# Hybrid GLA and GDN block: five GDN heads instead of six in the transposed form, the norm's row through GpSimd's queue, and its product a tick later

## The chip, the cores and the metric

The kernel runs on one core of a Trainium2 chip. The metric is the device time of one execution in microseconds (us), the median of several runs. One core has a matrix engine (TensorE, called PE below), a vector engine (VectorE, DVE), a scalar engine (ScalarE, ACT), GpSimd (POOL) and SyncE (SP). SP, ACT and POOL each issue DMAs, and 16 DMA engines move the bytes.

## The reference

The block computes, for one sequence of 1024 tokens of width 1024, a gated linear attention (GLA) of 4 heads and a gated delta rule (GDN) of 8 heads on the same normalised input, projects each with its own weight, merges the two by sigmoid gates, projects again, and ends with a squared-ReLU MLP. All is float32. What matters here is the end of the GDN part:

```python
def rms_norm(x, w):
    xf = x.astype(jnp.float32)
    y = xf * lax.rsqrt(jnp.mean(xf * xf, axis=-1, keepdims=True) + EPS)
    return (y * w.astype(jnp.float32)).astype(x.dtype)
...
    o_d = gated_delta_chunked(d_q, d_k, d_v.reshape(bsz, s, GDN_HEADS, GDN_DV), beta, g)
    o_d = rms_norm(o_d, gdn_onorm_w) * jax.nn.silu(d_g.reshape(bsz, s, GDN_HEADS, GDN_DV))
    y_d = o_d.reshape(bsz, s, GDN_V) @ w_branch_gdn
```

Each head's output o has 1024 tokens by 128 values. Its norm takes, for each token, the mean of the squares over the 128 values; then o is scaled, multiplied by the gate and given to the projection, which wants the values on the partitions and the tokens along the free axis.

## The kernel before, in words

**Matmuls.** PE carries nearly everything. A float32 product is split into a high and a low part (tiles with H and L in their names: hH, hL, wH, wL), and three matmuls take the place of one. `dense_b` (L477) makes one projection of 128 columns for all 1024 tokens: 8 k steps of 6 matmuls, accumulated in a tile pm of PSUM (128 x 1024). Small products go to tiles pa (128 x 512). The GLA projection, the gate projection and the GDN projection (`branch`, one after another) each make seven products P2, P1, P6, P7, P4, P5, P3 of sums of quarters, in the manner of Strassen. The weight's quarters are called A11, A12, A21 and A22, and the input's Q11 to Q22.

**The agenda.** A clock counts ticks: one after each k step of `dense_b`, and one after each two k steps of a `branch` product. `at(dt, fn)` (L373) puts a function on the agenda dt ticks later, and `tick` (L384) runs what is due. In a GDN head `on(t, fn)` counts from the head's first tick, and `last_on(t, fn)` puts the function behind everything else of that tick. PE, DVE and ACT execute what they are given in just this order. From head 7 on, POOL's instructions and SP's DMAs keep the order of the code too (the loop that calls `gdn_head`, L1852 on, sets `strict` for them); before that the scheduler places them by what they wait for.

**A GDN head.** `gdn_head(h)` (L909) takes 24 ticks: three `dense_b` (for q, v and the gate). It starts a recurrence over 8 chunks at tick 24 (`c0`, `c1`, `c2`: PE multiplies ke with the state st, ACT makes rs and vn, DVE makes the next st from decB and a pa tile), which lasts to about tick 48. So a head's tail runs on ticks 48 and later, beside the next heads' first projections, and head 7's recurrence runs beside the first products of the GLA projection. In the code, `begin` is the head's first tick, so tick 50 of head 5 is tick 2 of head 7.

**Two forms of the tail.** The flag `turned` (L979) chooses.

- Turned, heads 0 to 5: `c2` writes o with the values on the partitions, which is how the projection wants it. The sums over values are then sums over partitions: ACT squares (`half_squares`, ticks 48 and 50), DVE transposes in 32 x 32 blocks and reduces (`sums`, 53 and 56), the groups are added (`groups`, 59), and `roots` (62) makes 1024 reciprocal roots in a 32 x 32 tile sqt and stores them, 4 KB, to `on_d[h]` in DRAM. `rows` (66) reads them back as a broadcast to all 128 partitions: the tile row, 512 KB. `gated` (58) has multiplied o into the gate sg (the tile si), and `times` (71) multiplies sg by row on DVE. Three ticks behind, ACT's queue stores sg to `od_d` (512 KB).
- Not turned, heads 6 and 7: o has the tokens on the partitions. ACT squares with a running sum (`results`, ticks 35 and 47), PE and DVE make the token sums of q in another place (`token_total`, tick 32, with the constant quad; its columns vq at tick 33), `norm` (48) makes a column rs of 8 numbers a partition, `scale` (50) multiplies the tile ob, and `fin` (52, 53) turns ob by eight PE transposes (`pa<-ident,ob`), which DVE multiplies into sg. The store to `od_d` is on tick 56. For head 6 these ticks are moved back by `end` = 27 and more (L1076), for head 7 the last ones by 6.

**Load buffers.** Most tiles of 512 KB share one pool of 30 buffers, which are given out in rotation (tag w4, L24): row, si, ob, aacc's input araw, the xq and wq tiles, and others. A load into a buffer waits until the tile that was there before is done with.

**The GLA projection's loads.** `gla_plan` (L1653) lists ticks relative to the end of head 7: SP loads the weight quarter A12, then Q21, A11, Q11, Q12, Q22 (each xq pair 2 x 512 KB) and A21 (the tiles wq, 2 x 512 KB) on ticks -19 to -2, and A22 on tick 8. On tick 1 `add_w` adds A22 onto A21 in SBUF by two DMAs of POOL's queue, which must follow SP's load of A21. On ticks 8 and 10 DVE subtracts A11 from the sum (`raw<-wq,raw`). `w_neg` (ticks -9 to 2) fills the low halves of the weights, tiles wB, by four more DMAs of POOL's queue.

Of the kernel before, what the change touches and what calls it, by code (L numbers as in the profile page):

```python
# [50 lines left out]
def block_kernel(ctx: ExitStack, tc: tile.TileContext, x, c, ada_w, ada_b, pre_mix_w, post_mix_w,  # L51
# [15 lines left out]
    V, A, G, T = engines = [InOrder(tc, e) for e in (nc.vector, nc.scalar, nc.gpsimd, nc.tensor)]  # L67
    DMA, ST = InOrder(tc, nc.sync), nc.scalar
# [8 lines left out]
    def t4(shape=(128, 1024), dt=F32, p="t", tag="w4"):  # L77
        return w4.tile(list(shape), dt, tag=tag, name=nm(p), bufs=tag_bufs[tag])
# [7 lines left out]
    def dump(name, src, dst=None):  # L86
        if dbg and name in dbg:
            DMA.dma_start(dbg[name] if dst is None else dst(dbg[name]), src)


    def rsqrt(v, n, rt=None):

        if rt:
            r, t = rt
        elif n == 64:
            r, t = t4((128, n), p="rs"), t4((128, n), p="rt")
        else:
            r, t = small(n, "rs"), small(n, "rt")
        V.tensor_scalar(t.bitcast(I32), v.bitcast(I32), 1, None, ALU.logical_shift_right)
        V.tensor_scalar(r.bitcast(I32), t.bitcast(I32), -1.0, float(0x5F3759DF), ALU.mult, ALU.add)  # L100

        V.tensor_mul(t, r, r)
        V.tensor_mul(t, t, v)
        V.scalar_tensor_tensor(t, t, -10.0 / 3, t, ALU.add, ALU.mult)
        V.scalar_tensor_tensor(r, t, 5.0, r, ALU.add, ALU.mult)
        V.tensor_mul(t, r, r)
        V.scalar_tensor_tensor(t, t, -27.0 / 1024, v, ALU.mult, ALU.mult)
        last["rs"] = V.scalar_tensor_tensor(r, t, 9.0 / 16, r, ALU.add, ALU.mult).ins
        return r

    def small(n, p="s", bufs=3, dt=F32):
        return sm.tile([128, n], dt, tag=f"{p}{n}", name=nm(p), bufs=bufs)
# [260 lines left out]
    def at(dt, fn):  # L373
        agenda.append((clock[0] + dt, len(agenda) + uid[0] * 100000, fn))
        agenda.sort(key=lambda e: e[:2])
        uid[0] += 1
# [324 lines left out]
    def r3(t, n=8):  # L701
        return t.rearrange("p (t q) -> p t q", t=n)
# [203 lines left out]
    od_d = [dr.tile([2, 128, 1024], F32, name=f"od_d{i}") for i in range(4)]  # L906
    on_d = [dr.tile([1024], F32, name=f"on_d{h}") for h in range(8)]

    def gdn_head(h, then=None):  # L909
# [3 lines left out]
        def on(t, fn):  # L913
            at(begin + t - clock[0], fn)
# [38 lines left out]
        def conv_silu(ps, ct, t, late=0):  # L953

            y, u = t4(p="cv"), {}
            A.activation(y, ps, AF.Copy, scale=ccol[:, 3 * 24 + ct:3 * 24 + ct + 1])

            def tap(s_):
                V.scalar_tensor_tensor(y[:, s_:], ps[:, :S - s_], ccol[:, (3 - s_) * 24 + ct:(3 - s_) * 24 + ct + 1],
                                       y[:, s_:], ALU.mult, ALU.add)  # L960

            def tanh():
                u["t"] = t4(p="si")
                A.activation(u["t"], y, AF.Tanh)

            t += late
            for s_ in (1, 2, 3):
                on(t + s_, lambda s_=s_: tap(s_))
            on(t + 4, tanh)
            on(t + 6 - late, lambda: V.scalar_tensor_tensor(y, u["t"], 1.0, y, ALU.add, ALU.mult))  # L970
            return y
# [4 lines left out]
        psq = dense_b(h_rhs)  # L976

        q = conv_silu(psq, h, 8)
        z, turned = {}, h < 6  # L979
        vq = None if turned else small(8, "vq")  # L980

        def att(hf):
# [52 lines left out]
        c = {"st": None}  # L1035
# [81 lines left out]
        def sums(hf):  # L1117
            if not hf:
                c["t"] = t4(p="sqt")
            h_ = slice(hf * 512, (hf + 1) * 512)  # L1120
            V.transpose(c["t"][:, h_], c["sq"][:, h_])
            V.reduce_sum(so[:, hf * 16:(hf + 1) * 16], r3(c["t"][:, h_], 16), axis=mybir.AxisListType.X)
# [11 lines left out]
        def roots():  # L1134
            g = c["g"]
            V.transpose(g[5], rsqrt(g[0], 32, g[3:5]))
            DMA.dma_start(on_d[h].rearrange("(b i) -> b i", i=32), g[5])

        def rows():
            c["row"] = t4(p="row")  # L1140
            DMA.dma_start(c["row"], on_d[h].partition_broadcast(128))

        def gated():
            V.scalar_tensor_tensor(sg, c["ob"], don, sg, ALU.mult, ALU.mult)

        def times():
            V.tensor_mul(sg, sg, c["row"])
            on(74, lambda: A.dma_start(od_d[h // 2][h % 2], sg))
            dump("odT", sg, lambda t: t[h * 128:(h + 1) * 128, :])

        def last_on(t, fn):
            on(t, lambda: at(0, fn))
# [6 lines left out]
            then()  # L1159
        if turned:  # L1160
            for t, fn in ((48, lambda: half_squares(0)), (50, lambda: half_squares(1)), (53, lambda: sums(0)),
                          (56, lambda: sums(1)), (58, gated), (59, groups), (62, roots), (66, rows), (71, times)):
                last_on(t, fn)
        else:
            on(48 + end, norm)
            on(50 + end, scale)
            on(52 + f_, lambda: fin(0))
            on(53 + f_, lambda: fin(1))
        psg = dense_b(h_rhs)

        sg = t4(p="si")
# [1251 lines left out]
    for n in range(len(seq)):  # L2423
        gi, key, c = seq[n]
# [106 lines left out]
```

## Time and profile before

| | |
|---|---|
| runs | 1894.22, 1892.55, 1894.04 us; median 1894.04 |
| profiled execution | 1894.02 us |
| its span in the trace | 1892.3 us |
| mean granted clock of PE | 0.997 |
| PE busy | 1862.0 us, 98% of the span |
| DVE busy | 1393.2 us, 74% |
| ACT busy | 887.7 us, 47% |
| POOL busy | 150.4 us, 8% |

The profiled execution took 1.7 us more than its span, the time outside the first and the last instruction. An engine that is busy for a smaller share may still be what PE waits for at one place. Row by row, a line of the profile gives a start, a duration, the engine, the operation, what it writes and reads, and in brackets how long the engine had been idle before and what ended the wait. Nearly all rows have the line L38, that of the helper which records every operation (`InOrder`), so the tiles' names tell the place. Tiles that matter: st, ke, rs, vn (the recurrence of a head), row and on_d (the norm's row), si (the gate), ob (a head's output), xq and wq (input and weight quarters of the GLA projection), raw (a whole weight piece), sl (the merge's gates, read from DRAM beside A22), wB (split weights), od_d (a head's result in DRAM).

### The profile page before, as it was taken

How to read it: one execution, taken by the hardware profiler on the slowest of the kernel's cores; microseconds unless marked ns; L12 is line 12 of the kernel's file. 1: busy time of each engine (PE TensorE's matmuls, PEld its weight loads, DVE VectorE, ACT ScalarE, POOL GpSimd, SP SyncE). 2: the span in 40 equal slices, each digit the busy share in tenths (PEclk: the TensorE clock that was granted, in tenths of full speed). 3: DMA queues.
4: the chain of work that ended last, by engine and by line, in shares of the span. 5: the costliest groups of instructions: out<-in, count | busy, mean ns of one | idle time of the engine just before them, and what ended most of it. 6: DMA issues, size and time to landing. Idle time of an engine off the chain costs nothing. (4 is left out here: it accounts for less than half of the span.)

```text
span 1892.3 us, 26295 instructions
## 1 busy us (share of the span) xinstructions
PE 1862.0 (98%) x10109; PEld 1558.6 (82%) x10109; DVE 1393.2 (74%) x2163; ACT 887.7 (47%) x1535; POOL 150.4 (8%) x138
## 2 busy tenths in 40 slices
PE   7999999999999999999999999999999999999998
PEld 5788888989898888888878888878888888888886
DVE  6664834868766677777879778976788877777887
ACT  5574324252333444444654555568644446433333
POOL 2120110010110000000101001000022220000001
PEclk9999999999999999999999999999999999999999
DMA  9695563223125445554859666246667668252425
GB/s 314 216 257 181 161 145 102 68 84 118 56 80 156 126 144 144 143 152 160 243 157 243 196 160 197 80 154 221 220 209 232 235 213 317 72 222 104 163 100 100
DMA packets 253469, 314.32 MB, mean 166 GB/s; under 512 B 72898, under 2 KB 178576, under 8 KB 253344
## 3 DMA queue, kind: packets, MB, share of 16 engines
q1 hardware_dynamic: 223616, 277.84, 45.6%
q0 software_dynamic: 13456, 19.80, 6.0%
q10 hardware_dynamic: 16272, 15.02, 2.4%
q8 instruction: 79, 1.29, 0.3%
q14 instruction: 46, 0.38, 0.1%
HBM read 232.19 MB, written 80.41 MB: 165 GB/s over the span
## 5 line engine op out<-in xcount | busy, mean ns | idle before, releaser
L38 PE MATMUL pm<-hH,wH 128*128 128x512 f32 x864 | 286.0, 412 | 0.0
L38 PE MATMUL pm<-hL,wH 128*128 128x512 f32 x864 | 269.1, 393 | 0.0
L38 PE MATMUL pm<-hH,wL 128*128 128x512 f32 x864 | 267.1, 390 | 0.0
L38 PE MATMUL pm<-oH,wB 128*128 128x512 f32 x672 | 215.4, 395 | 0.0
L38 PE MATMUL pa<-w,yH 128*128 128x512 f32 (+1 forms) x696 | 212.3, 387 | 0.0
L38 PEld LDWEIGHTS pm<-hH,wL 128*128 128x128 f32 x864 | 162.1, 188 | 36.9
L38 PEld LDWEIGHTS pm<-hL,wH 128*128 128x128 f32 x864 | 162.1, 188 | 35.9
L38 PEld LDWEIGHTS pm<-hH,wH 128*128 128x128 f32 x864 | 145.1, 190 | 17.0
L38 DVE TENSOR_TENSOR w<-raw,w 128x512 fp32r<-128x512 f32 (+1 forms) x144 | 125.8, 876 | 42.0 <-ACT w L38 38.6
L38 PEld LDWEIGHTS pa<-w,yH 128*128 128x128 f32 x696 | 130.1, 188 | 26.9 <-DVE ya L38 0.4
L38 PEld LDWEIGHTS pm<-oH,wB 128*128 128x128 f32 x672 | 126.8, 189 | 25.8
L38 ACT CAST w<-raw 128x512 fp32r<-128x512 f32 (+1 forms) x144 | 99.5, 712 | 89.1 <-DVE raw L38 80.0
L38 PE MATMUL pa<-w,yL 128*128 128x512 f32 (+1 forms) x348 | 134.5, 387 | 0.0
L38 PE MATMUL pm<-oL,wB 128*128 128x512 f32 x336 | 131.3, 391 | 0.0
L38 PE MATMUL pa<-oB,w 128*128 128x512 f32 x480 | 113.4, 394 | 2.2 <-ACT oB L38 1.2
L38 ACT CAST wH<-raw 128x1024 fp32r<-128x1024 f32 x62 | 64.4, 1046 | 99.7 <-PE pm L38 57.6
L38 PEld LDWEIGHTS pa<-oB,w 128*128 128x128 f32 x480 | 90.9, 190 | 22.0 <-ACT oB L38 1.6
L38 DVE SCALAR_TENSOR_TENSOR cv<-pm,ccol,cv 128x1023 f32<-128x1023 f32 (+2 forms) x72 | 92.0, 1278 | 13.7 <-ACT cv L38 12.6
L38 DVE TENSOR_TENSOR wL<-raw,wH 128x1024 fp32r<-128x1024 f32 x62 | 75.3, 1218 | 34.1 <-ACT wH L38 33.9
L38 PE MATMUL pm<-oT,w 128*128 128x512 f32 x384 | 90.8, 389 | 0.0
L38 PE MATMUL pa<-oT,w 128*128 128x512 f32 x384 | 90.8, 389 | 0.0
L38 DVE TENSOR_TENSOR ya<-pa,ya 128x512 f32<-128x512 f32 (+1 forms) x83 | 56.0, 683 | 43.7 <-PE pa L38 43.7
(419 smaller groups left out, 3726.8 us busy)
## 6 DMA issues: line engine op xcount, KB each, us to landing
yL<-y_d SPq DMA_DIRECT2D x53, 512.0 KB, 7.6
raw<-in_mlp_w_dram SPq DMA_DIRECT2D x23, 1024.0 KB, 6.1
raw<-in_w_in_dram SPq DMA_DIRECT2D x18, 1024.0 KB, 6.9
raw<-in_w_in_dram SPq DMA_DIRECT2D x32, 512.0 KB, 5.0
araw<-in_ada_w_dram SPq DMA_DIRECT2D x32, 512.0 KB, 3.8
raw<-in_mlp_w_dram SPq DMA_DIRECT2D x18, 512.0 KB, 4.5
araw<-in_ada_w_dram SPq DMA_DIRECT2D x32, 256.0 KB, 6.3
sl<-sg_d SPq DMA_DIRECT2D x16, 512.0 KB, 7.3
```

The source lines that it names most:

```text
L38: r = fn(*args, **kw)
```

## The change

Three edits. Head 5 takes the form that is not turned, so heads 0 to 4 are turned. The store of the 4 KB row to `on_d` and the broadcast load of row, both on SP's queue before, are issued by POOL. The product with row moves from tick 71 to 72, and the store of the result from tick 74 to 75.

```diff
-        z, turned = {}, h < 6
+        z, turned = {}, h < 5
...
             V.transpose(g[5], rsqrt(g[0], 32, g[3:5]))
-            DMA.dma_start(on_d[h].rearrange("(b i) -> b i", i=32), g[5])
+            G.dma_start(on_d[h].rearrange("(b i) -> b i", i=32), g[5])
...
             c["row"] = t4(p="row")
-            DMA.dma_start(c["row"], on_d[h].partition_broadcast(128))
+            G.dma_start(c["row"], on_d[h].partition_broadcast(128))
...
             V.tensor_mul(sg, sg, c["row"])
-            on(74, lambda: A.dma_start(od_d[h // 2][h % 2], sg))
+            on(75, lambda: A.dma_start(od_d[h // 2][h % 2], sg))
...
-                          (56, lambda: sums(1)), (58, gated), (59, groups), (62, roots), (66, rows), (71, times)):
+                          (56, lambda: sums(1)), (58, gated), (59, groups), (62, roots), (66, rows), (72, times)):
```

The tail of head 5 now uses `late` = 0 and `end` = 0, so its `norm` is on tick 0 of head 7, `scale` on 2, `fin` on 4 and 5, and its `od_d` store on tick 8. How the orders of the engines change shows at three places.

SP's queue before, at the end of head 7 (raw is A11, on_d and row are those of head 5, xq are Q11, Q12 and Q22, wq the two halves of A21):

```order
L38 DMA raw_8389<-in_w_branch_gla_dram 128x4x512
L38 DMA on_d_490<-sqt_8238 32x32
L38 DMA araw_8460<-in_ada_w_dram 128x1024
L38 DMA row_8508<-on_d_490 128x1024
L38 DMA xq_8521<-oa_d_477 128x2x512
L38 DMA xq_8523<-oa_d_478 128x2x512
L38 DMA xq_8541<-oa_d_477 128x2x512
L38 DMA xq_8543<-oa_d_478 128x2x512
L38 DMA xq_8559<-oa_d_479 128x2x512
L38 DMA xq_8561<-oa_d_480 128x2x512
L38 DMA wq_8576<-in_w_branch_gla_dram 128x4x256
L38 DMA wq_8577<-in_w_branch_gla_dram 128x4x256
```

The same place now:

```order
L38 DMA raw_8414<-in_w_branch_gla_dram 128x4x512
L38 DMA araw_8474<-in_ada_w_dram 128x1024
L38 DMA xq_8533<-oa_d_477 128x2x512
L38 DMA xq_8535<-oa_d_478 128x2x512
L38 DMA xq_8553<-oa_d_477 128x2x512
L38 DMA xq_8555<-oa_d_478 128x2x512
L38 DMA xq_8571<-oa_d_479 128x2x512
L38 DMA xq_8573<-oa_d_480 128x2x512
L38 DMA wq_8588<-in_w_branch_gla_dram 128x4x256
L38 DMA wq_8589<-in_w_branch_gla_dram 128x4x256
```

The store of head 5's row and its load are gone, and araw follows raw at once. The rows of the heads 0 to 4 have left SP's list as well.

POOL's queue before, from its last memset in the GDN part on (wB and wq belong to the GLA projection):

```order
L38 MEMSET U_5471 128x1024
L38 DMA wB_8418<-in_w_branch_gla_dram 128x4x256
L38 DMA wB_8489<-in_w_branch_gla_dram 128x4x256
L38 DMA wB_8564<-in_w_branch_gla_dram 128x4x256
L38 DMA wq_8576<-in_w_branch_gla_dram 128x4x256
L38 DMA wq_8577<-in_w_branch_gla_dram 128x4x256
```

The same place now, with the rows of the heads 3 and 4 and what stands around them:

```order
L38 DMA on_d_488<-sqt_7433 32x32
L38 DMA row_7678<-on_d_488 128x1024
L38 DMA on_d_489<-sqt_7835 32x32
L38 DMA row_8090<-on_d_489 128x1024
L38 DMA wB_8443<-in_w_branch_gla_dram 128x4x256
L38 DMA wB_8503<-in_w_branch_gla_dram 128x4x256
L38 DMA wB_8576<-in_w_branch_gla_dram 128x4x256
L38 DMA wq_8588<-in_w_branch_gla_dram 128x4x256
L38 DMA wq_8589<-in_w_branch_gla_dram 128x4x256
```

Ten DMAs, a store and a load for each of the five heads, stand ahead of the first wB.

DVE before, at the start of head 7 (cv and wL belong to the projection, si with row is head 4's product, si with pm is a gate):

```order
L38 TENSOR_TENSOR wL_8117<-raw_7985,wH_8065 128x1024
L38 SCALAR_TENSOR_TENSOR cv_8049<-si_8115,cv_8049 128x1024
L38 TENSOR_TENSOR si_7351<-si_7351,row_8079 128x1024
L38 SCALAR_TENSOR_TENSOR aacc_7145<-araw_8037,sc,aacc_7145 128x1024
L38 SCALAR_TENSOR_TENSOR si_8154<-si_8154,pm_8052 128x512
L38 TENSOR_TENSOR wL_8204<-raw_8129,wH_8176 128x1024
L38 STREAM_TRANSPOSE sqt_8214<-qj_8028 128x512
```

The same place now, from the last operation of head 5's norm on (ob is head 5's output):

```order
L38 SCALAR_TENSOR_TENSOR rs_8163<-rt_8164,rs_8163 128x8
L38 SCALAR_TENSOR_TENSOR aacc_7145<-araw_8048,sc,aacc_7145 128x1024
L38 TENSOR_TENSOR si_7351<-si_7351,row_8090 128x1024
L38 TENSOR_TENSOR ob_7950<-ob_7950,rs_8163 128x1024
L38 SCALAR_TENSOR_TENSOR si_8180<-si_8180,pm_8063 128x512
L38 TENSOR_TENSOR wL_8230<-raw_8140,wH_8202 128x1024
L38 STREAM_TRANSPOSE sqt_8245<-qj_8039 128x512
```

Eleven small operations of head 5's norm, of which the last is shown, and aacc stand ahead of head 4's product, and the scaling of ob behind it. PE before, four ticks into head 7 (st with ke, rs with U and vn with kt are head 6's recurrence, the rows with hH and hL a k step of the projection):

```order
L38 MATMUL pa_8198<-st_8185,ke_7884 128x128
L38 MATMUL pm_8165<-hH_559,wH_8065 128x512 x2
L38 MATMUL pm_8165<-hL_574,wH_8065 128x512 x2
L38 MATMUL pm_8165<-hH_559,wL_8117 128x512 x2
L38 MATMUL pa_8198<-rs_8201,U_5469 128x128
L38 MATMUL pm_8165<-hH_610,wH_8065 128x512 x2
L38 MATMUL pm_8165<-hL_626,wH_8065 128x512 x2
L38 MATMUL pm_8165<-hH_610,wL_8117 128x512 x2
L38 MATMUL pa_8198<-vn_8219,kt_7880 128x128
```

The same place now, with the transposes of ob:

```order
L38 MATMUL pa_8223<-st_8212,ke_7887 128x128
L38 MATMUL pm_8191<-hH_559,wH_8076 128x512 x2
L38 MATMUL pm_8191<-hL_574,wH_8076 128x512 x2
L38 MATMUL pm_8191<-hH_559,wL_8128 128x512 x2
L38 MATMUL pa_8240<-ident,ob_7950 128x128 x4
L38 MATMUL pa_8223<-rs_8226,U_5469 128x128
L38 MATMUL pm_8191<-hH_610,wH_8076 128x512 x2
L38 MATMUL pm_8191<-hL_626,wH_8076 128x512 x2
L38 MATMUL pm_8191<-hH_610,wL_8128 128x512 x2
L38 MATMUL pa_8262<-ident,ob_7950 128x128 x4
```

The groups `pa<-ident,ob` stand ahead of the recurrence's matmuls of that tick.

## The prediction

> **What bounds the kernel now.** I read the page's busy times first, then the waits of PE over the whole span, then the timeline around the longest of them.
>
> ```profile
> PE 1862.0 (98%) x10109; PEld 1558.6 (82%) x10109; DVE 1393.2 (74%) x2163; ACT 887.7 (47%) x1535; POOL 150.4 (8%) x138
> PE pa L38 <- DVE st L38: 4.4, 3, 3.7
> ```
>
> PE is busy for 98% of the span, so time can come only from fewer or faster matmuls, or from the 2% in which PE stands. Of that 2% one wait of 3.7 us on the tile st is the largest after the start of the program. It stands here:
>
> ```profile
> 953.22 0.27 PE L38 MATMUL pa<-ident,cv 128*128 128x128 f32 x1
> 957.19 0.49 PE L38 MATMUL pa<-st,ke 128*128 128x128 f32 x2 [3.70 <-DVE st L38]
> ```
>
> This is the last GDN head's recurrence (ticks 48 and later of head 7), which runs inside the GLA branch's first two products. The windows of 2 us right behind it show a second cost:
>
> ```profile
> 958.00:960.00 2.00, 1.85 (x6) 0.99 (x5) 2.00 (x3) 1.74 (x10) 0.00 (x0) 0.55 0.00 0
> 960.00:962.00 2.00, 2.00 (x7) 1.69 (x8) 1.77 (x2) 0.52 (x2) 0.00 (x0) 0.59 0.00 0
> 962.00:964.00 2.00, 2.00 (x14) 1.73 (x13) 1.21 (x2) 0.00 (x0) 0.00 (x0) 1.00 0.00 0
> ```
>
> The third number from the end is the granted clock: 0.55 and 0.59, then 1.00. So (0.45 + 0.41) x 2 = 1.72 us of matmul work is lost after the wait. The stop costs 3.70 + 1.72 = 5.4 us in all.
>
> Why is st late? DVE runs its instructions in a fixed order, and something ahead of st came late:
>
> ```profile
> 951.41 1.23 DVE L38 TENSOR_TENSOR raw<-wq,raw 128x1024 f32<-128x1024 f32 x1 [4.88 <-DMA wq<-in_w_branch_gla_dram]
> 956.79 0.35 DVE L38 SCALAR_TENSOR_TENSOR st<-st,decB,pa 128x128 f32<-128x128 f32 x1
> ```
>
> DVE idled 4.88 us for a DMA into wq and needed 5.38 us from there to st, with no further gap. That DMA is GpSimd's adding DMA: it adds the weight quarter A22 onto A21, which SP must have loaded before.
>
> ```profile
> 942.21 2.69 POOL L38 DMA_DIRECT2D wq<-in_w_branch_gla_dram  x2 [10.88 <-DMA wq<-in_w_branch_gla_dram]
> 944.38 1.83 POOL L38 DMA_DIRECT2D wB<-in_w_branch_gla_dram  x1
> ```
>
> GpSimd waited 10.88 us for the load of A21. So the chain is: SP's load of A21, GpSimd's add, DVE's product with raw, st, PE. I then read how the load of A21 comes to be late: SP's issues, SP's waits, and the DMA queues from 910 to 944 us.
>
> ```profile
> 915.66 1.27 SPq L38 DMA_DIRECT2D araw<-in_ada_w_dram  x1
> 918.56 0.32 SPq L38 DMA_DIRECT2D row<-on_d  x1
> 920.16 7.15 SPq L38 DMA_DIRECT2D xq<-oa_d  x6
> 927.40 1.06 SPq L38 DMA_DIRECT2D wq<-in_w_branch_gla_dram  x2
> ```
>
> ```profile
> SPq L38 <- DMA od_d<-si: 5.6, 1, 5.6
> SPq L38 <- DVE sqt L38: 4.1, 1, 4.1
> ```
>
> ```profile
> q1 hardware_dynamic: 4125, 7.13, 60.3%
> q10 hardware_dynamic: 144, 0.52, 3.9%
> wq<-in_w_branch_gla_dram SPq DMA_DIRECT2D x4, 512.0 KB, 14.2
> ```
>
> A load of 512 KB into wq takes 14.2 us in the median here: it is queued behind what SP issued before it. Two of the things ahead belong to head 5's norm: its row (512 KB, read back at 918.56), and SP's wait of 4.1 us for the tile sqt, ahead of the 4 KB store of that row, which holds back araw. A third, the store od_d of head 5 by ACT's queue, held SP's next load of wq for 5.6 us.
>
> **The change part by part.** The profiled execution took 1894.02 us, and the median of the runs is 1894.04, so the sum against the one holds for the other.
>
> *Work added to PE.* Head 5 leaves the transposed form, so its output must be turned by PE: two groups of four transposes, and one matmul with quad for the token sums. Heads 6 and 7 show the price:
>
> ```profile
> 993.98 0.60 PE L38 MATMUL pa<-ident,ob 128*128 128x128 f32 x4
> 994.34 0.47 PE L38 MATMUL pm<-oH,wB 128*128 128x512 f32 x1
> 897.54 0.30 PE L38 MATMUL pa<-sqr,quad 128*128 128x32 f32 x2
> 897.68 0.47 PE L38 MATMUL pa<-vn,kt 128*128 128x128 f32 x2
> ```
>
> From start to next start it is 0.36 us for a group and 0.14 for the quad pair: 2 x 0.36 + 0.14 = 0.86 us, all on the path, since PE is full.
>
> *The load of A21.* (a) Head 5's row is gone. In the 34 us from 910 to 944 queue q1 moved 7.13 MB in 60.3% of the engines' time, 20.5 us, or 2.88 us per MB; 0.52 MB is 1.5 us. (b) The wait of 4.1 us is gone, so araw goes out up to 4.1 us earlier, when the engines are partly idle. The window ahead has a DMA share of 0.44:
>
> ```profile
> 910.00:914.00 4.00, 3.47 (x21) 2.69 (x20) 3.86 (x9) 3.79 (x8) 0.00 (x0) 1.00 0.44 140
> ```
>
> About half of araw's 1.5 us then falls into idle engines: 0.75 us, bounds 0 and 1.5. (c) The row also took one of the rotating load buffers; without it each xq load takes the buffer that is released one step sooner. Where the engines are full an earlier issue brings nothing; I take 0.3 us, between 0 and one step of 7.15 / 6 = 1.2 us. (d) Head 5's od_d store moves forward by some 38 us, to tick 8 of head 7. On q10 it took 3.9% of 34 us = 1.3 us. But the load of A22 that waited 5.6 us for it comes forward too and competes; I take half, 0.7 us, bounds 0 and 1.3. Sum: 1.5 + 0.75 + 0.3 + 0.7 = 3.25 us earlier. All taken at their lower bounds, and the row's 1.5 us lost to the A22 load that now comes sooner, give 0; all at their upper bounds give 5.5, of which only 3.70 can be used. GpSimd's add and its wB DMA, which stand behind A21 in GpSimd's queue, move with it.
>
> *The stop of PE.* 3.70 - 3.25 = 0.45 us is left. Next late is the wB DMA, which PE needs with the third matmul behind the stop, and which moves by the same amount. The lost clock, 1.72 us, goes if the stop is short. How short it must be the profile of before does not say well, but one other place limits it, two waits in a row and the window behind them:
>
> ```profile
> 1260.43 0.50 PE L38 MATMUL pa<-oB,w 128*128 128x512 f32 x1 [1.17 <-ACT oB L38]
> 1261.69 2.68 PE L38 MATMUL pa<-oB,w 128*128 128x512 f32 x6 [0.76 <-DVE oB L38]
> 1262.00:1266.00 4.00, 4.00 (x12) 3.12 (x11) 4.00 (x5) 3.22 (x8) 0.00 (x0) 0.57 0.00 0
> ```
>
> 1.17 + 0.76 = 1.93 us of standing within 3 us also brought the clock to 0.57. I therefore take the loss as gone under about 1.9 us of stop, that is from a shift of 1.8 us on.
>
> The Trainium skill, page "TensorE: Matmul & The Clock Gate", section "What's actually happening", says that the array drops to half its rate after at least one idle window of about 3.4 us; by it the loss would go as soon as the stop is under 3.4 us, from a shift of 0.3 us on. The rows at 1260 speak against so high a limit.
>
> *The row through GpSimd's queue.* Heads 0 to 4 keep their row. Its price on that queue is not in the trace, but a broadcast of the same 512 KB is: the tile gr, loaded by GpSimd, beside the tile row, loaded by SP (minimum, median, maximum to landing):
>
> ```profile
> DMA to landing us min/median/max: 2.6/5.6/11.1
> DMA to landing us min/median/max: 3.4/4.7/5.4
> ```
>
> So the row comes some 0.9 us later (bounds: 2.8 earlier, 6.4 later). The cover, in the heads 0 to 3:
>
> ```profile
> 697.54 1.23 DVE L38 TENSOR_TENSOR si<-si,row 128x1024 f32<-128x1024 f32 x1 [1.68 <-DMA row<-on_d]
> 702.88 0.69 DVE L38 SCALAR_TENSOR_TENSOR si<-si,pm 128x512 f32<-128x512 f32 x1 [2.92 <-ACT si L38]
> 706.55 0.35 DVE L38 SCALAR_TENSOR_TENSOR st<-st,decB,pa 128x128 f32<-128x128 f32 x1
> 708.30 0.38 PE L38 MATMUL pa<-st,ke 128*128 128x128 f32 x2
> ```
>
> The product must end by 702.88, so the row may land by 701.65, 4.1 us later than now; behind that, st has 708.30 - 706.90 = 1.4 us of room before PE needs it. The tick that the product is moved puts aacc ahead of it on DVE, and the store od_d behind it on ACT's queue a tick later, so that ACT does not stand for it. Cost: 0, up to (6.4 - 5.5) = 0.9 us a head. The same rows say what the removed waits of DVE for the row were worth: nothing, as DVE idles 2.92 us for ACT right after. GpSimd's queue held no work between its memsets and the first wB DMA, so nothing there is delayed by waiting for sqt.
>
> The Trainium skill, page "DMA: Bandwidth & Descriptors", section "SWDGE vs HWDGE vs iDMA", speaks against the move: descriptors of GpSimd's queue are made by software and have the slower setup (its table of figures has about 1 us to the first byte against 0.6). By those figures, an estimate, the row would come 0.4 us later; that too is under the cover, and no run here shows the two queues at one transfer yet.
>
> *Head 5's norm at head 7's start.* Behind the squares on ACT, DVE does 11 small operations, aacc, head 4's product and the scaling of ob, before PE's first group of transposes at tick 4:
>
> ```profile
> 882.69 0.59 ACT L38 COPY ob<-pa 128x512 f32<-128x512 f32 x1 [1.57 <-PE pa L38]
> L38 ACT ACTIVATE ob<-pa x12: 268/278/295, 943.0 to 979.9; 128x128 f32<-128x128 f32 x12
> 980.35 0.17 DVE L38 TENSOR_SCALAR so<-so 128x8 f32<-128x8 f32 x1 [4.17 <-ACT ob L38]
> 982.47 1.22 DVE L38 TENSOR_TENSOR xq<-xq,xq 128x1024 f32<-128x1024 f32 x1
> 882.46 1.22 DVE L38 TENSOR_TENSOR si<-si,row 128x1024 f32<-128x1024 f32 x1 [0.58 <-DMA row<-on_d]
> 890.54 0.38 PE L38 MATMUL pa<-rs,U 128*128 128x128 f32 x2
> ```
>
> 882.69 + 4 x 0.28 = 883.8; + 2.1 (980.35 to 982.47) = 885.9; three operations of 1.2 = 889.5; PE is there at 890.5. So 1.0 us of room, and cost 0, with a bound of 0.8 us if the head-4 row lands 6.4 us later than now (the product then starts at 888.9 instead of 885.9 + 1.2 = 887.1, 1.8 us later, of which 1.0 is room). DVE's other work for head 5 shrinks: its transposes, sums and roots go, and it is not the bound.
>
> *Sum.* 0.86 - 3.25 - 1.72 = -4.1 us: 1894.0 - 4.1 = **1889.9 us**. With the shift between 1.8 and 3.7 us it is -2.7 to -4.6: 1889.4 to 1891.3.
>
> **The rivals.** *The load comes hardly sooner.* The engines are full, and the A22 load and the sl tiles that are set free fill the room of the row. Shift 0 to 1.8, clock still lost: +0.9 to -0.9, 1893.1 to 1894.9, say 1894.0. For it: the 14.2 us are mostly six xq loads, which stay. Against it: 0.5 MB less ahead is 0.5 MB less.
>
> *The same, with the clock kept.* If a stop of 1.9 to 3.7 us leaves the clock alone, the same small shift gives +0.86 - 0.9 - 1.72 = -1.8: 1892.3 us. The limit named above from the Trainium skill, page "TensorE: Matmul & The Clock Gate", would make it so for most of these stops; the rows at 1260 speak against it.
>
> *Slower: GpSimd's row lands too late in every head.* If the landing is over 4.7 + 5.5 = 10.2 us, DVE stands at the product, the gate and st come late, and PE waits in each of the heads. On top of the forecast it is 0.9 x 4 + 0.8 = 4.4 us at a landing of 11.1 us, 1894.3, and 2.8 x 4 + 2.7 = 13.9 us at 13 us, 1903.8. It is slower than before from about 11 us on, and by over 0.2% from about 11.8. For it: gr had 11.1 once, and this row is read back right behind a store through the same queue. Against it: that was one of four loads back to back.
>
> *The new transposes wait.* Head 5's chain at head 7's start comes 2 us later than I have it, PE stands 1 to 2 us at tick 4 on top of the forecast: 1889.9 + 1.5 = 1891.4.
>
> *DVE's waits for the row were worth something.* Were the stalls of DVE for the row felt by PE, each head would gain up to 1.68: 1885 or so. The 2.92 us of idle time after speak against it.
>
> **How the numbers follow.** A measurement of this kernel can tell about 0.2%, 3.8 us, from no change, which is near the forecast's own size. The forecast's case has 0.56: 0.41 of it beyond 3.8 us, 0.15 within. Hardly sooner 0.14, the same with the clock kept 0.08, the transposes 0.07: all within 0.2%. The late row 0.12, slower by over 0.2%. DVE's waits 0.03, faster. So faster 0.44, same 0.15 + 0.14 + 0.08 + 0.07 = 0.44, slower 0.12. The range goes from the forecast's lower end less 1 us for the spread of the runs (1892.55 to 1894.22), 1888.4, to the upper end of the load that comes hardly sooner plus as much, 1895.9; what is left out is the late row and DVE's waits.
>
> **What would show it.** In the profile after: PE's longest wait for st near 956 us under 1 us, no window at 0.55 behind it, GpSimd's add issued some 3 us earlier against PE's work, two groups of transposes at 890 us without an idle time before them, and DVE's product with the row followed by idle time for ACT as before. The forecast is wrong if the wait for st is still over 2 us, if PE waits for ob at tick 4 of head 7, or if st waits appear in the heads 2 to 6 behind a late row.

## The result and the profile after

The changed kernel takes 1889.38 us in the median of 18 runs (1887.93 to 1892.13), the kernel before 1894.14 us in the median of 18 runs beside them. The ratio is 0.9976, with a 95% interval of 0.9968 to 0.9983, so 3.2 to 6.1 us are gained, 4.5 in the middle. The profiled execution of the changed kernel took 1887.93 us, the fastest of its 18, with a span of 1886.2; its difference to the profile of before, 6.1 us, is therefore larger than the typical one.

PE's waits over the whole span of the changed kernel show that the wait of 3.7 us for st is gone, and that what is left of st is one wait of 0.5 (at 942.16, where the kernel before waits 0.59):

```profile
PE pm L38 <- DVE x L38: 9.9, 1, 9.9
PE pa L38 <- ACT oB L38: 1.2, 1, 1.2
PE pa L38 <- DVE oB L38: 1.1, 2, 0.8
...
PE pa L38 <- DVE st L38: 0.5, 1, 0.5
```

The timeline of the same kernel at the place of the stop, DVE first. The product with raw starts 0.32 us after DVE became free, not 4.88, and at 946.80 instead of 951.41:

```profile
946.80 1.23 DVE L38 TENSOR_TENSOR raw<-wq,raw 128x1024 f32<-128x1024 f32 x1 [0.32 <-DMA wq<-in_w_branch_gla_dram]
...
952.27 0.35 DVE L38 SCALAR_TENSOR_TENSOR st<-st,decB,pa 128x128 f32<-128x128 f32 x1
```

On PE the matmul that waited has no bracket any more, and the windows behind it have the full clock (third number from the end):

```profile
953.26 0.39 PE L38 MATMUL pa<-st,ke 128*128 128x128 f32 x2
```

```profile
954.00:956.00 2.00, 1.77 (x9) 1.21 (x9) 2.00 (x2) 1.39 (x7) 0.00 (x0) 1.00 0.00 0
956.00:958.00 2.00, 2.00 (x14) 1.74 (x13) 1.81 (x4) 0.34 (x2) 0.00 (x0) 1.00 0.00 0
```

Up the chain, GpSimd issues its two additions of A22 at 936.17 and 939.49, six and four microseconds before the 942.21 and 943.63 of the kernel before; the first waited 4.89 us instead of 10.88 for SP's load.

```profile
936.17 1.27 POOL L38 DMA_DIRECT2D wq<-in_w_branch_gla_dram  x1 [4.89 <-DMA wq<-in_w_branch_gla_dram]
939.49 1.27 POOL L38 DMA_DIRECT2D wq<-in_w_branch_gla_dram  x1 [2.05 <-PE pm L38]
```

And SP's issues: araw follows raw at once, and the six loads of xq begin at 918.06 instead of 920.16. The load of A21 itself is issued only 0.43 us earlier than before (927.40), but its two halves land at 935.54 and 938.93 instead of 941.63 and 943.09.

```profile
909.64 0.38 SPq L38 DMA_DIRECT2D raw<-in_w_branch_gla_dram  x1
910.07 0.51 SPq L38 DMA_DIRECT2D araw<-in_ada_w_dram  x1
918.06 8.80 SPq L38 DMA_DIRECT2D xq<-oa_d  x6
926.97 1.89 SPq L38 DMA_DIRECT2D wq<-in_w_branch_gla_dram  x2
```

Where the time went is best read by following one kind of matmul, `pa<-st,ke`, which stands in both programs equally often. The table has its start in both profiled executions, and from 1262 us on an operation `y<-pm,y` of DVE:

| place | before | after | difference | step since the row above |
|---|---|---|---|---|
| head 6, early | 842.87 | 842.79 | -0.08 | |
| behind the quad matmul | 853.53 | 853.67 | +0.14 | +0.22 |
| head 7, ahead of the transposes | 888.93 | 889.04 | +0.11 | 0 |
| behind the transposes | 894.32 | 895.31 | +0.99 | +0.88 |
| head 7, later | 920.53 | 920.49 | -0.04 | -1.03 |
| ahead of the stop | 947.92 | 947.87 | -0.05 | 0 |
| behind the stop | 957.19 | 953.26 | -3.93 | -3.88 |
| behind the lost clock | 964.54 | 959.18 | -5.36 | -1.43 |
| output projection | 1262.68 | 1257.34 | -5.34 | 0 |
| MLP | 1419.23 | 1412.88 | -6.35 | -1.01 |

Three lines of it were in the forecast: PE's added work, the stop, and the clock behind it. Two were not: 1.03 us given back between 894 and 920 us, and 1.01 us behind 1262. The second belongs to this execution and not to the change, as the section on the second lost clock shows.

### The profile page after: what moved, and what is told of

Its sections match the earlier page's. It is cut to its first block, busy times and chain, and to the rows that moved or that the text cites. A ratio compares the mean times of both kernels' runs of the same rounds, so it can differ in the third digit from the quotient of the medians.

```text
span 1886.2 us, 26335 instructions
## 1 busy us (share of the span) xinstructions
PE 1860.3 (99%) x10119; PEld 1558.7 (83%) x10119; DVE 1389.2 (74%) x2157; ACT 888.4 (47%) x1549; POOL 157.6 (8%) x148
```

## The experiments

Each kernel ran beside the kernel before on the same chip; the ratio is to that, and 0.9976 is the changed kernel. Each ratio is uncertain by about 0.0009, which is 1.7 us.

| run | edit | median us | ratio | 95% interval | longest wait for st behind 950 us |
|---|---|---|---|---|---|
| e1 | five heads only | 1889.44 | 0.9975 | 0.9965 to 0.9984 | 1.5 |
| e2 | queue and tick only | 1892.43 | 0.9994 | 0.9985 to 1.0002 | 2.0 |
| e9 | five heads and queue, no tick | 1889.11 | 0.9977 | 0.9967 to 0.9987 | none |
| e3 | before, A21 ahead of Q22 | 1893.85 | 0.9996 | 0.9987 to 1.0005 | none, 3.1 at 944.6 |
| e4 | after, row put back on SP | 1891.45 | 0.9987 | 0.9978 to 0.9996 | 2.2 |
| e5 | after, store of head 5 late | 1894.07 | 1.0000 | 0.9991 to 1.0008 | 3.1 |
| e11 | after, other store's bytes | 1890.06 | 0.9977 | 0.9967 to 0.9987 | 0.8 |
| e12 | after, sg's buffer held | 1893.91 | 0.9996 | 0.9987 to 1.0005 | 2.9 |
| e6 | after, DVE work back | 1888.62 | 0.9973 | 0.9962 to 0.9984 | none |
| e10 | four heads | 1889.16 | 0.9977 | 0.9967 to 0.9987 | none |
| e8 | after, row's load on tick 70 | 1888.70 | 0.9973 | 0.9963 to 0.9982 | none |
| e0 | before again, one profile | 1893.57 | | | 3.2 |

### Which of the three edits

```diff
e1_five_heads, against before
-        z, turned = {}, h < 6
+        z, turned = {}, h < 5
```

> Only the first edit: five heads in the transposed form; the rows stay on SP's queue, the product on tick 71. Theory (the gain is head 5's own: its row, SP's wait for it and DVE's work for it are gone from head 7's end): the whole gain, 4 to 5 us less than before, about 1889.5, and no wait of PE for st over 0.6 us near 955 us. Rival (the gain comes from taking the rows off SP's queue): at most a third of it, 1 to 2 us less than before, and a wait for st of 2 us or more remains.

```diff
e2_queue_and_tick, against the changed kernel
-        z, turned = {}, h < 5
+        z, turned = {}, h < 6
```

> Only the other two edits: six heads in the transposed form, the row's store and load on GpSimd's queue, product on tick 72. Theory (head 5's own work): head 5's row is still loaded ahead of A21, only SP's wait of 4.1 us is gone, so A21 comes about 0.8 us sooner and PE still waits 2 to 3.7 us for st with half the clock behind it: 0 to 2 us less than before. It may be slower by up to 2 us, since GpSimd's store of head 5's row now waits for sqt ahead of the second wB transfer. Rival (the queue is what counts): 4 to 5 us less than before.

```diff
e9_tick_71, against the changed kernel
-                          ... (66, rows), (72, times)):
+                          ... (66, rows), (71, times)):
-            on(75, lambda: A.dma_start(od_d[h // 2][h % 2], sg))
+            on(74, lambda: A.dma_start(od_d[h // 2][h % 2], sg))
```

> The changed kernel with the product with row back on tick 71 and the store on 74: first and second edit without the third. Theory (DVE idles for ACT behind the product anyway): no change against the changed kernel, 1889.4 within 1 us. Rival (the row on GpSimd's queue comes too late for tick 71, and the third edit is needed): DVE stands 1 to 2 us more a head ahead of aacc, and PE feels some of it: 1 to 5 us slower.

e1 has the whole gain: 1889.44 us, 0.9975. So the first edit is the change, and the second and third add nothing that these runs can tell apart from nothing. e1 alone is not quite as the theory had it: its profile, of an execution of 1890.08 us, still shows a wait of 1.5 us for st, where 0.6 was the limit. e9 agrees that the tick is not needed: DVE stands longer for the row than in the changed kernel (10.4 us in five waits, against 4.2 in four), and the time is the same, since DVE idles for ACT behind it as before (2.17 us behind the first product).

e2 is within its interval of no change. Its profile shows two waits for st, of 2.1 and 2.0 us, where before had one of 3.7. The first is new, and it is the late row: with six heads, head 5's row goes through GpSimd's queue right behind a wB transfer, lands 10.6 us after its issue, and DVE stands at the product and is then late for the next st.

```profile
933.23 1.22 DVE L38 TENSOR_TENSOR si<-si,row 128x1024 f32<-128x1024 f32 x1 [2.05 <-DMA row<-on_d]
...
942.59 0.34 DVE L38 SCALAR_TENSOR_TENSOR st<-st,decB,pa 128x128 f32<-128x128 f32 x1
```

```profile
942.98 0.49 PE L38 MATMUL pa<-st,ke 128*128 128x128 f32 x2 [2.13 <-DVE st L38]
```

So the second edit belongs with the first one: with head 5's row on it, GpSimd's queue would have been the wrong place.

### Is it the load of A21

```diff
e3_a21_earlier, against before (gla_plan)
-             (-4, "load_x", Q12), (-3, "load_x", Q22), (-2, "load_w", A21), (1, "add_w", A21, A22), ...
+             (-4, "load_x", Q12), (-3, "load_w", A21), (-3, "load_x", Q22), (1, "add_w", A21, A22), ...
```

> The kernel before with one line changed: SP loads the weight quarter A21 ahead of the input quarter Q22 instead of behind it. Theory (PE's wait for st is the late A21 and nothing else): 1 MB is taken from in front of it, at 2.88 us per MB A21 lands about 3 us sooner, the wait of 3.7 us shrinks to under 1 us and the clock stays, so about 4.5 us less than before, 1889.6, though six heads are transposed. If Q22 becomes the late one instead, the DVE subtractions on xq wait for up to 3 us and the gain is lost. Rival (st is late by DVE's own load in head 7): no change.

```diff
e4_row_put_back, against the changed kernel
             on(53 + f_, lambda: fin(1))
+            if h == 5:
+                last_on(66, lambda: DMA.dma_start(t4(p="row"), on_d[4].partition_broadcast(128)))
```

> The changed kernel with one load added that nothing reads: SP loads a row of 512 KB where head 5's row stood, behind araw and ahead of xq. Theory (the row's bytes and its buffer in front of A21 are the largest part): A21 lands about 1.8 us later than in the changed kernel, of 4.6 us won at the add's landing 2.8 stay, PE's wait for st is 1 to 2 us, 1 to 3 us slower than the changed kernel: 1890.4 to 1892.4. Rival (the gain is the wait for sqt, the store od_d, or DVE's work, and the row is hidden): like the changed kernel, 1889.4.

e3 gains nothing clear (0.9996), in the way that its expectation named as the miss. A21 came sooner, its additions were issued at 934.78 and 936.70, and the wait for st at 957 us is gone. But Q22 is now late, DVE's subtraction waits for it, and PE waits 3.14 us for st two chunks sooner, with a lost clock behind it:

```profile
943.10 1.23 DVE L38 TENSOR_TENSOR xq<-xq,xq 128x1024 f32<-128x1024 f32 x1 [1.43 <-DMA xq<-oa_d]
944.24 0.34 DVE L38 SCALAR_TENSOR_TENSOR st<-st,decB,pa 128x128 f32<-128x128 f32 x1
```

```profile
944.63 0.80 PE L38 MATMUL pa<-st,ke 128*128 128x128 f32 x2 [3.14 <-DVE st L38]
```

That speaks against the rival that DVE's own load makes st late, and it says that this order of the loads is not the remedy: in e3 the DMA share is 1.03 to 1.17 in each stretch of 8 us from 918 to 950, and one load or another is last.

e4 puts one load back and takes 2.1 us of the gain (1891.45 against 1889.38), as expected. PE waits 2.2 us for st, and two windows show the lost clock, (0.12 + 0.31) x 4 = 1.72 us:

```profile
PE pa L38 <- DVE st L38: 2.2, 1, 2.2
952.00:956.00 4.00, 1.78 (x8) 1.29 (x8) 3.91 (x7) 1.15 (x3) 0.00 (x0) 0.88 0.30 47
956.00:960.00 4.00, 4.00 (x15) 3.20 (x14) 3.83 (x4) 2.31 (x12) 0.00 (x0) 0.69 0.00 0
```

The row's bytes and its buffer come back together in e4. Its xq loads go out singly (918.12 and 919.72, against 918.06 and 918.53 in the changed kernel), which the next section finds again where a buffer alone is held, so the run does not say that the bytes count.

### The store, its bytes and its buffer

```diff
e5_late_store, against the changed kernel
-                on(56 + f_, lambda: (DMA if h == 7 else A).dma_start(od_d[h // 2][h % 2], sg))
+                on(74 if h == 5 else 56 + f_, lambda: (DMA if h == 7 else A).dma_start(od_d[h // 2][h % 2], sg))
```

> The changed kernel with one line more: the store od_d of head 5 stays on tick 74, where it was before, instead of tick 56. Theory (term d of the forecast): the store competes again with A21 in the last 7 us of its load, and SP's load of A22 waits for it again; the two nearly cancel, A21 lands 0 to 1.3 us later and PE's wait for st grows by as much: 0 to 1.3 us slower than the changed kernel, 1889.4 to 1890.7. Rival (the freed A22 load is what the gain hangs on): 2 us slower or more.

This was the surprise: 1894.07 us, ratio 1.0000. With head 5 out of the transposed form, its row gone and its DVE work gone, one store left on its old tick takes back the whole gain. PE waits 3.1 us for st. The theory's price, 0 to 1.3 us, was far too low; the rival's was met, but whether by its cause is open, for the store keeps two things, its bytes beside A21, and the buffer of sg, which can't be given out before the store has read it. Two more runs tell them apart.

```diff
e11_store_traffic, against the changed kernel
             on(53 + f_, lambda: fin(1))
+            if h == 5:
+                on(74, lambda: A.dma_start(spare_d, U.rearrange("p t c -> p (t c)")))
...
e12_buffer_held, against the changed kernel
             on(53 + f_, lambda: fin(1))
+            if h == 5:
+                on(74, lambda: A.copy(small(8, "held"), sg[:, 0:8]))
```

> The changed kernel with one store added that nothing reads: on tick 74 of head 5, where its store od_d was before, ACT's queue writes 512 KB of another tile (U) to a spare place in DRAM. Head 5's own store stays on tick 56, so its buffer comes free as early as in the changed kernel. It tells apart why the late store took back the whole gain. Theory (the buffer: sg held until the store has landed moves every later load one place on in the order in which buffers come free, and makes A22 wait): 0 to 1.3 us slower than the changed kernel, 1889.4 to 1890.7. Rival (the store's bytes beside A21): 3 us slower or more, 1892.4 and above.

> The counterpart: the changed kernel with one small ACT copy added on tick 74 that reads 8 columns of sg and that nothing uses. The store stays on tick 56; only sg's buffer is held until tick 74. Theory (the buffer): xq's loads go out singly and later as in the kernel with the late store, A21 lands 2 us or more later, PE's wait for st is back at 1.5 to 3 us: 1.5 to 4 us slower than the changed kernel, 1890.9 to 1893.4. Rival (the store's bytes): like the changed kernel, 1889.4.

It is the buffer. e11, with 512 KB stored at the same time from another tile, has the ratio of the changed kernel, 0.9977, and its profile waits of 0.8 us for st at the stop and of 0.4 us for split weights (wB). e12 stores nothing more and only reads eight columns of sg on tick 74, and is back at 1893.91 us, 0.9996. The added copy itself takes little of ACT's time (the next instruction starts 0.10 us behind it), and e5 loses as much without it. Its wait for st is 2.9 us, and the clock is lost over a longer stretch, (0.03 + 0.50 + 0.32) x 4 = 3.4 us:

```profile
956.70 0.80 PE L38 MATMUL pa<-st,ke 128*128 128x128 f32 x2 [2.91 <-DVE st L38]
952.00:956.00 4.00, 1.79 (x10) 1.21 (x8) 3.93 (x8) 1.05 (x1) 0.00 (x0) 0.97 0.62 98
956.00:960.00 4.00, 3.30 (x9) 2.72 (x10) 3.97 (x5) 2.94 (x11) 0.00 (x0) 0.50 0.00 0
960.00:964.00 4.00, 4.00 (x18) 3.39 (x17) 2.13 (x4) 0.52 (x2) 0.00 (x0) 0.68 0.00 0
```

How can one buffer do that? The traces don't name buffers, but the times at which loads go out tell what they waited for. In the changed kernel xq's first two loads are issued at 918.06 and 918.53, right behind PE's last reads of hL and hH in the first k step of head 7's last projection, which end at 918.03 and 918.48. In e12 the first is issued at 918.85, right behind hH of that step (918.82), and the second at 920.44, right behind hL of the second step (920.41): with sg held, each load gets the next buffer in line. A22's second half is issued at 935.34, when the copy that reads sg has ended (935.31), so it got the buffer of sg itself:

```profile
935.09 0.22 ACT L38 COPY held<-si 128x8 f32<-128x8 f32 x1
```

In the first 8 us of the rush less is moved for it (last number, GB/s): 295 in the changed kernel, and 224 in e12.

```profile
918.00:926.00 8.00, 8.00 (x46) 6.67 (x45) 6.22 (x8) 4.33 (x7) 1.30 (x1) 1.00 1.06 295
```

```profile
918.00:926.00 8.00, 8.00 (x45) 6.71 (x44) 5.89 (x7) 5.19 (x8) 1.30 (x1) 1.00 0.96 224
```

(295 - 224) GB/s x 8 us is 0.57 MB, one whole load less. But e1 shows that this is not the whole account. Its xq loads are issued as early as in the changed kernel (918.19 and 918.68) and it moves 284 GB/s in the same window, and yet A21's halves land at 939.21 and 941.12, as late as in e12 (939.29 and 941.32). What differs behind that is the additions: they land at 949.25 and 951.90 in e1, and at 950.89 and 953.49 in e12, where A22's second half went out 2.1 us later. PE then stood for 1.50 us in e1 and kept its clock, and for 2.91 us in e12 and lost 3.4 us of it. So the runs show what the held buffer costs and that it shifts the loads; by which of the shifted loads it makes st late is open.

### The microsecond that was given back

```diff
e6_dve_work_back, against the changed kernel
             on(53 + f_, lambda: fin(1))
+            if h == 5:
+                for t in (58, 59):
+                    last_on(t, lambda: V.tensor_tensor(c["ob"], c["ob"], c["ob"], ALU.add))
```

> The changed kernel with two DVE operations of 1.2 us added on ticks 58 and 59 of head 5 (ob added to itself, which nothing reads), about what gated and groups took there. The trace of after shows that PE's work for head 5's transposes, 1.07 us, is given back between 906 and 920 us, where PE had waited for ACT behind DVE. Theory (DVE's work of the transposed tail caused that wait): the give-back goes, PE stands up to 1 us more between 906 and 920, 0.5 to 1.2 us slower than the changed kernel: 1889.9 to 1890.6. Rival (the give-back has another cause): like the changed kernel, 1889.4, and PE is still on time at 920 us.

The theory fell. e6 takes 1888.62 us, ratio 0.9973, and its matmuls `pa<-st,ke` come 1.04 us closer to those of before between 906.1 (1.58 us behind) and 920.5 (0.54 behind): the give-back is there with DVE's work put back. What the profile of before shows at the place is a wait of ACT. It stood 1.50 us before it could write the tile si:

```profile
908.80 1.07 ACT L38 ACTIVATE si<-cv 128x1024 f32<-128x1024 f32 x1 [1.50 <-PE pa L38]
909.77 0.35 ACT L38 ACTIVATE vn<-pa,ksC 128x128 f32<-128x128 f32 x1
```

```profile
908.51 0.22 PE L38 MATMUL pa<-uw 64*64 64x64 f32 x1
913.50 0.68 PE L38 MATMUL pa<-cv,kT 128*128 128x128 f32 x4 [0.52 <-ACT rs L38]
```

By these times that si got the buffer of uw, which PE reads last at 908.51 (until 908.73), so vn was late, and PE stood for rs at 913.50. In the changed kernel si finds its buffer free, ACT writes it at 907.81 without a wait, and PE does not stand at 913.5:

```profile
907.81 1.05 ACT L38 ACTIVATE si<-cv 128x1024 f32<-128x1024 f32 x1
```

So this looks like a buffer again, shifted by the tiles that head 5 no longer takes. It agrees with the other profiles: ACT does not wait there in e1 and e6 (907.95 and 908.40), and waits 1.90 us in e2, which has six heads as before. But no run changed that one buffer by itself, and of the 1.03 us only 0.52 show as a wait of PE.

```diff
e10_four_heads, against the changed kernel
-        z, turned = {}, h < 5
+        z, turned = {}, h < 4
```

> The changed kernel with h < 4 instead of h < 5: head 4 loses the transposed form too. Theory (a head without it costs PE 0.86 to 1.07 us, and the gain belonged to the place of head 5, beside the GLA projection's loads): 0.5 to 1.1 us slower than the changed kernel, 1889.9 to 1890.5, if nothing at head 6 was waiting for the row's work. Rival (each head taken out of the form gains): 2 us or more below it.

e10 is like the changed kernel, 1889.16 us and 0.9977. The expected loss of 0.5 to 1.1 us lies inside what the interval (1.9 us to either side) can tell, so the run shows that taking head 4 out gains nothing that can be told, and leaves open whether it costs its microsecond.

### A late row, and the second lost clock

```diff
e8_rows_late, against the changed kernel
-                          ... (62, roots), (66, rows), (72, times)):
+                          ... (62, roots), (70, rows), (72, times)):
```

> The changed kernel with the row's load on tick 70 instead of 66, so that it lands some 6.5 us later in each of the heads 0 to 4: the rival of a late row, made on purpose. The forecast put the room at 5.5 us over the usual landing: 4.1 us until DVE's next instruction and 1.4 us until PE needs st. Theory: DVE stands 2 to 3 us at the product in each head, PE about 1 us in the heads 0 to 3 and 1 to 2 us at head 5's transposes: 4 to 7 us slower than the changed kernel, 1893.4 to 1896.4. Rival (PE never feels DVE's wait for the row): like the changed kernel, 1889.4.

The edit did not do what it was meant to: the five loads of a row are issued within 0.4 us of the same times in both kernels (the first at 693.22 and 693.56), and the row lands 3.6 to 6.1 us after it (medians 5.4 in e8 and 4.6). Ahead of head 7 the load goes out when its buffer is free, whatever tick it is written on. The run says nothing on the room that I had worked out; e2 is the only one in which a row was late.

e0 is the kernel before once more, with a second profile.

> The kernel before, unchanged, for a second profile of it. The first one had two places with half the clock, at 958 and at 1262 us; in the profiles with head 5 taken out or moved the second is missing although PE waits there just as long (1.2 and 0.8 us). Theory (whether a wait of about 1.9 us halves the clock depends on where it falls): this profile may have it or not; the first place, behind a wait of 3.7 us, has it again. Rival (the second place belongs to the kernel before): it has it again at the same strength, 0.5 in 1262 to 1264.

It has both lost clocks again, the wait for st being 3.2 us this time. The second place is behind two waits of PE for oB, which are equal in all kernels, some 1.16 and 0.77 us. The rows of the kernel before again, of e8, and of the changed kernel:

```profile
1260.10 0.49 PE L38 MATMUL pa<-oB,w 128*128 128x512 f32 x1 [1.15 <-ACT oB L38]
1261.36 4.83 PE L38 MATMUL pa<-oB,w 128*128 128x512 f32 x13 [0.77 <-DVE oB L38]
```

```profile
1254.57 0.50 PE L38 MATMUL pa<-oB,w 128*128 128x512 f32 x1 [1.17 <-ACT oB L38]
1255.83 12.54 PE L38 MATMUL pa<-oB,w 128*128 128x512 f32 x47 [0.76 <-DVE oB L38]
1256.00:1260.00 4.00, 4.00 (x11) 3.17 (x12) 4.00 (x5) 3.36 (x9) 0.00 (x0) 0.58 0.00 0
```

```profile
1255.08 0.50 PE L38 MATMUL pa<-oB,w 128*128 128x512 f32 x1 [1.16 <-ACT oB L38]
```

Behind these equal waits the clock is lost in seven of the fourteen profiles and kept in seven. It is lost in before, e0, e5 and e12, with the first matmul at 1260.1 to 1260.8 (in e0 the clock is 0.68 and 0.90 in the windows of 4 us from 1260 on), and also in e8, e6 and e11, at 1254.57, 1256.08 and 1256.69. It is kept in the changed kernel, e9, e10, e1, e4, e2 and e3, at 1255.08 to 1258.64. So the loss belongs neither to the old kernel, nor to the waits' length, nor to the place in the program.

The traces show what decides. In the kernel before the half clock lasts from 958.21 to 961.62 and from 1261.99 to 1265.41, 3.41 us each time, and the two starts are 303.78 us apart, which is 89 steps of 3.413 us. The clock's first rise in that profile, at 12.72 us, is 277 steps ahead of the first start. In all nine profiles with a lost clock the changes lie on such a grid, counted from the first rise, and that rise is elsewhere in each execution (12.7 to 16.0 us). Cut into windows by its grid, a profile shows for each window its length, how long PE was busy (the next number), and which clock came after it (third number from the end of the row below). The first pair of rows is e11, the second e10:

```profile
1254.30:1257.72 3.42, 1.73 (x7) 0.88 (x5) 1.05 (x1) 3.42 (x7) 0.00 (x0) 1.00 0.00 0
1257.72:1261.12 3.40, 3.17 (x8) 2.49 (x9) 3.40 (x4) 3.40 (x10) 0.00 (x0) 0.50 0.00 0
```

```profile
1253.88:1257.29 3.41, 1.77 (x7) 0.91 (x5) 1.00 (x1) 3.41 (x7) 0.00 (x0) 1.00 0.00 0
1257.28:1260.70 3.42, 3.12 (x14) 2.61 (x15) 3.42 (x4) 3.42 (x10) 0.00 (x0) 1.00 0.00 0
```

PE stood for 3.42 - 1.73 = 1.69 us of the window in e11 and for 3.41 - 1.77 = 1.64 in e10. Between 20 and 1870 us of the fourteen profiles there are thirteen windows at the full clock in which PE stood for 1.69 us or more, and half the clock followed each of them; in every other it stood for 1.64 us or less, and the clock stayed. So it is the standing within one window that counts. The two waits at 1260 sum to 1.93 us, but a window's border can part them, and where the border falls is chance. About 1 us of what the profile of after has won comes from there.

## Why the prediction was right, and where its steps were not

The forecast was 1889.9 us, and 1889.38 was measured. The mechanism is as it was put: A21's chain comes sooner, PE's stop for st goes, and the lost clock with it. That the number is so near is in part luck: work that was priced too low was given back at another place, and the terms of A21's load, some far too small, cover one stop that none can exceed. The steps one by one:

*Work added to PE, 0.86 us.* It was 0.22 + 0.88 = 1.1 us. But the words "all on the path, since PE is full" failed: PE stood later in the same head, behind ACT, and gave 1.03 us back. A busy share of 98% hid a wait of 0.52 us; the rest of the 1.03 us shows as no wait.

*The load of A21, 3.25 us.* The additions landed 4.6 and 3.1 us sooner (946.77 and 950.98, against 951.39 and 954.04), enough for all of the stop, which went from 3.70 to nothing in this execution; in e1's profile 1.5 us remain. The sum was near, its terms were not. (a) and (c) together, the row's bytes and its buffer, were put at 1.8 us of shift; in e4 the additions land 2.7 and 1.1 us later than in the changed kernel (949.44 and 952.11), and the time is 2.1 us longer, where its profile also has 1.72 us of lost clock. (d), the store that moves forward: I priced its bytes and a waiting load at 0.7 us of shift, with 1.3 as the end; in e5 the additions land 3.6 and 3.1 us later (950.40 and 954.08), and with the clock that this loses the time is 4.7 us longer (1894.07 against 1889.38). In e11 the bytes move the additions by 0.9 and 1.7 us, and its ratio is that of the changed kernel; e12 puts the buffer at 4.5 us by the medians, and at 3.8 by the ratios. The step that failed is the one on buffers, "I take 0.3 us, between 0 and one step of 1.2 us": it saw the row's buffer, but not that head 5's own gate tile comes free 37 us sooner, and it took an earlier issue to be worth next to nothing where the engines are full. Since the terms each cover the same stop, they don't add up.

*(b), SP's wait for sqt.* araw did follow raw at once, as forecast. e2 has this without the removed head, and lies between 0.4 us lost and 2.8 gained, with another wait in it; the term alone was not measured.

*The clock, 1.72 us.* At the stop it was 1.43 us of PE's time, in the expected place. The limit that I drew from the rows at 1260, about 1.9 us of stop, gave the right answer for the changed kernel, but it is not a limit on the length of a stop: stops of 2.0 and 2.1 us cost no clock in e2, where a window's border parts each of them (1.20 and 1.26 us, 0.95 and 1.18), and 2.2 us did in e4, with 2.02 of it in one window. The limit lies between 1.64 and 1.69 us within one window. On the rule of the Trainium skill, page "TensorE: Matmul & The Clock Gate", section "What's actually happening": that half the rate comes after at least one idle window of about 3.4 us is not so here, since a window in which PE stood for 1.69 us of 3.41 sufficed (e11). That the window runs freely agrees with the traces, whose grids begin elsewhere in each execution. Its length agrees with the sums of lost clock: 1.72 us is one window at half rate, and 3.4 us in e12 is two.

*The row through GpSimd's queue, at no cost.* It landed in 3.6, 4.6 and 5.8 us (minimum, median, maximum), against 3.4, 4.7 and 5.4 on SP's: no slower. The setup that the Trainium skill, page "DMA: Bandwidth & Descriptors", section "SWDGE vs HWDGE vs iDMA", has against this queue doesn't show at this size. The rival of the late row shows only with a loaded queue (10.6 us in e2). DVE's waits for the row were worth nothing that can be told, as forecast (e9).

*Head 5's norm at head 7's start.* The scaling of ob ended at 889.65 (889.5 forecast), and PE came to the transposes at 890.67 without a wait:

```profile
888.43 1.22 DVE L38 TENSOR_TENSOR ob<-ob,rs 128x1024 f32<-128x1024 f32 x1
```

```profile
890.67 0.60 PE L38 MATMUL pa<-ident,ob 128*128 128x128 f32 x4
```

*The other rivals.* A load that comes hardly sooner is what e5 and e12 look like, and the changed kernel would have looked so had its store stayed on the old tick.

No version of these runs is clearly better than the changed kernel: e6, e8 and e9 lie within 0.8 us of it, inside the intervals.

## What to carry to other kernels

Where tiles come from one rotating pool, a change that takes a tile away, or lets it go sooner, moves the buffer of every request behind it; follow that list, not only the instructions that the diff names, and look at what each load of a crowded stretch waits for. When many loads compete, putting one of them first can make another last (e3). And a wait of PE costs more than its length if the clock falls behind it, and whether it falls can be the chance of one execution, so compare several profiles before a microsecond of that is put down to the edit.

## What was not expected of the hardware

The time from issue to landing of one and the same kind of load depends on what is in front of it and beside it far more than on its queue: a broadcast of 512 KB through GpSimd's queue took 3.6 to 5.8 us with the queue empty, and 10.6 us behind a wB transfer in the crowded stretch of e2, where SP's xq loads of 512 KB took up to 8.7 us as well. The clock is lost in portions of one window: 3.41 us at half rate, 1.71 us of work, at the stop once in before, e0, e3 and e4, and twice in e5 and e12. PE need not stand for the whole window; 1.69 us of it sufficed, and 1.64 us did not.
